# A hybrid encoder layer on one core: re-splitting weights at each use instead of parking the split pair, one weight load for both attentions' up products, one merged attention kept on chip

## The chip, the cores and the metric

The kernel runs on one core of one Trainium2 chip. The metric is device time in microseconds (us) of one execution. All figures below come from one profiled execution and from three runs of the kernel before.

## The reference, cut

Two sequences (`x_prompt`, `x_sample`; each 512 tokens by 1024 channels) go through the same layer:

```python
def encoder_layer(x, ...):
    x = x + 0.5 * swiglu(rms_norm(x, ffn1_norm), ...)           # 1024 -> 2816 -> 1024
    proj = rms_norm(x, mix_norm) @ w_in                         # one joint input projection
    aq, ak, av, mq, mk, mv, gate_pre, o_pre, g_att, g_mlstm = split(proj)
    att = gqa_block_attention(rope(norm(aq)), rope(norm(ak)), av)        # 8 heads of 64, width 512
    mem = mlstm_bidirectional(mq, mk, mv, gate_pre, ..., o_pre, head_norm)  # 4 heads of 128, width 512
    merged = sigmoid(g_att) * (att @ w_up_att) + sigmoid(g_mlstm) * (mem @ w_up_mlstm)
    x = x + merged @ w_out                                      # 1024 -> 1024
    x = x + 0.5 * swiglu(rms_norm(x, ffn2_norm), ...)
    return x
# trunk: one such layer, then rms_norm(x, final_norm)
```

All data are fp32. The change lies between the last part of the joint projection and the start of the second FFN: memory heads, the two "up" products, the merge, the output product.

## The kernel before, in words

**Precision.** Every fp32 operand of a product is split into a high and a low float32r half. A product over K blocks of 128 is then three matmuls for each block (high x high, high x low, low x high). Splitting a weight block takes one ScalarE (ACT) copy (L213, or L265 in the FFN), and one VectorE (DVE) subtraction (L214 or L266).

**Stages.** FFN1 and the joint projection treat both sequences together, by a seven-product scheme of the Strassen kind: sums of weight blocks (`gu_left_a`, `gu_left_b`, `gu_left_c`) are multiplied by sums of activations (`xc`, made by `right_sums`). So does the second FFN. Its first products (L307 into `mm` and others) need the split gate block (L265, L266) and `xc`; L315 and L322 empty them. Between these stages the mixer treats the two sequences one after the other: `m0` and `m1`, objects of the class `Mixer`. Its steps:

- A memory head is `mem_head` (scores at L1178, exponentials at L1192, products with the values at L1231) and `mem_out` (transposes at L1223, squares, the norm). The norm's sums go through transposes on PE (L177), two short steps on GpSimd (POOL; L165, L167, which gives `rs`), and PE again, which spreads `rs` over the partitions (L187). Each head reads four tables of exponents from HBM (`box` from `ebuf`, L1137), to which POOL adds a mask for the first sequence (L1141).
- `merge_att(d)`: for each of eight blocks of 128 output channels, 12 matmuls of `w_up_att` with the attention (L731), then (1 + gate row) times that product (L1099), written to `mgbuf` in HBM (L1100).
- `merge_mem(d)`: 12 matmuls of `w_up_mlstm` with the memory; the gated result is added to the row read back from `mgbuf`, and split.
- `out_unit(d)`: 24 matmuls of `w_out`; the residual row comes from `xbuf` (L1249), is added (L1250) and written to `x2buf` (L1251). Beside the second sequence's out units, `prep2` reads the first sequence's `x2buf` rows (L1496), norms them (L628), writes them to `xnbuf` (L1498) and splits them into `xc` (L252, L253).

**Weights.** `load_w` is called twice for each up and out block, once for each sequence, with the same key. The first call fetches the raw block (512 KB), splits it, and writes both halves to HBM (`wpark`, 2 x 512 KB, L236). The second call reads both halves back (L228). Raw blocks share four buffers, split pairs four others.

**Order.** A unit is a pair (load, comp); `go` and `fill` issue a unit's load some units ahead of its products. A queue of units is filled in between the steps of the memory heads by `between()`. A table, `pace = 0, 12, 30`, says how many units are to be out after the first and after the second 24 of these steps. The queue holds one leftover of the joint projection, eight `merge_att` of `m0`, eight of `m1`, eight `merge_mem` of `m0`, eight `out_unit` of `m0`. Then follow eight `merge_mem` and eight `out_unit` of `m1`, then the FFN's first fetch. A scheduler orders instructions by priority (`shifted` changes it), after which each engine works through its own list in order. All large DMAs are issued by SyncE (SP), also in order.

Of the kernel before, what the change touches and what calls it, by code (L numbers as in the profile page):

```python
# [8 lines left out]
F32 = mybir.dt.float32  # L9
# [3 lines left out]
ALU = mybir.AluOpType  # L13
# [3 lines left out]
P = 128  # L17
S = 512
D = 1024
KD = D // P  # L20
# [6 lines left out]
def encoder(ctx, tc, I, outs):  # L27
    nc = tc.nc
# [90 lines left out]
    def f(ap):  # L119
        return ap.bitcast(F32)  # L120
# [16 lines left out]
    def A(shape, dtype=F32, name="a"):  # L137
        return apool.tile(shape, dtype, tag="a", name=nm(name))
# [82 lines left out]
    def load_w(view, key, ahead=60):  # L221


        if key in parked:
            d, shape = parked[key]
            w2 = wpool.tile(shape, F32R, tag="w8", bufs=4, name=nm("w"))
            for i in range(2):
                nc.sync.dma_start(f(w2[:, i]), d[:, i])  # L228
            return w2[:, 0], w2[:, 1]
        raw = fetch_w(view)  # L230
        with shifted(-ahead):
            hi, lo = split_w(raw, V_)
        shape = [P, 2] + list(raw.shape[1:])
        parked[key] = d, _ = dpool.tile(shape, F32, name=nm("wpark")), shape
        for i, t in enumerate((hi, lo)):
            nc.sync.dma_start(d[:, i], f(t))  # L236
        return hi, lo
# [3 lines left out]
    V_ = nc.vector  # L241
# [480 lines left out]
    def proj(view, key, src, n, done):  # L722

        return (lambda: load_w(view, key)), (lambda w: done(proj_w(*w, src, n)))

    def proj_w(wh, wl, src, n, p=None):
        p = p or MM()
        for k in range(n):
            sh, sl = src(k)
            for i, (a, b) in enumerate(((wh, sh), (wh, sl), (wl, sh))):  # L730
                nc.tensor.matmul(p, a[:, k, :], b, start=(k == 0 and i == 0), stop=(k == n - 1 and i == 2))  # L731
        return p
# [109 lines left out]
            if between:  # L842
                between()
    vbuf = [dpool.tile([P, 2, 4, S], F32, name=f"vbuf{s}") for s in range(2)]
    mgbuf = [dpool.tile([P, KD, S], F32, name=f"mgbuf{s}") for s in range(2)]
    abuf = [dpool.tile([P, 4, 2, S], F32, name=f"abuf{s}") for s in range(2)]

    class Mixer:
# [224 lines left out]
        def up_unit(self, part, d, src, done, bank=None, extra=None):  # L1073
            def load():
                if d % 2 == 0:
                    wv = I[("w_up_att", "w_up_mlstm")[part]][0].rearrange("(k p) c -> p k c", p=P)
                    self.wups[part, d // 2] = load_w(wv[:, :, d * P:(d + 2) * P], ("up", part, d))
                if extra:
                    extra()

            def comp(_):
                wu = self.wups[part, d // 2]
                cl = slice((d % 2) * P, (d % 2 + 1) * P)
                done(proj_w(wu[0][:, :, cl], wu[1][:, :, cl], lambda k: (src()[:, k, 0, :], src()[:, k, 1, :]), 4,
                            bank and bank()))
            return load, comp

        def load_att(self):
            self.att = A([P, 4, 2, S], F32R, "att")
            nc.sync.dma_start(f(self.att), abuf[self.s])  # L1090

        def gate_row(self, g, d):
            t = self.ths[g, d] = T2()
            nc.sync.dma_start(t, mgbuf[self.s][:, d, :] if g == "g" else J[0].buf[self.s][g, d])

        def merge_att(self, d):
            def done(pu):
                t = self.ths.pop(("a", d))
                V_.scalar_tensor_tensor(t, t, 1.0, pu, op0=ALU.add, op1=ALU.mult)  # L1099
                nc.sync.dma_start(mgbuf[self.s][:, d, :], t)  # L1100
            return self.up_unit(0, d, lambda: self.att, done, None, lambda: self.gate_row("a", d))

        def merge_mem(self, d):
            def done(pu):
# [6 lines left out]
            return self.up_unit(1, d, lambda: self.mem, done, (PS, PT)[d % 2], lambda: [self.gate_row(g, d) for g in "mg"])  # L1111

        def mem_fetch(self, h):
            qk = self.qks[h] = []
# [129 lines left out]
        def out_unit(self, d, acc, after=None):  # L1244
            s = self.s

            def done(pp):
                xt = T2(F32, "f2")
                nc.sync.dma_start(xt, xbuf[s][:, d, :])  # L1249
                V_.scalar_tensor_tensor(xt, pp, 0.5, xt, op0=ALU.mult, op1=ALU.add)  # L1250
# [5 lines left out]
            return proj(wov[:, :, d * P:(d + 1) * P], ("out", d), lambda k: (self.mh[:, k, :], self.ml[:, k, :]), KD,  # L1256
                        done)

    pin = tc.keep_in_program_order
# [192 lines left out]
    m0.mem_fetch(1)  # L1452
    queue.append((lambda: None, lambda _: j.rest(13)))
    m0.load_att()
    queue.extend(m0.merge_att(d) for d in range(KD))
    m1.load_att()
    queue.extend(m1.merge_att(d) for d in range(KD))
    acc2 = [None, None]
    heads = [(m, h) for m in (m0, m1) for h in range(HM)]
    step = [0]  # L1460
    pace = 0, 12, 30

    def between():
        i, n = divmod(step[0], 24)
# [46 lines left out]
    W += [up.left(j) for j in (1, 2)]  # L1511
# [140 lines left out]
```

## Time and profile before

| | |
|---|---|
| three runs: median (lowest to highest) | 2092.08 us (2089.03 to 2097.18) |
| the profiled execution: time, span | 2092.42 us, 2090.6 us |
| granted TensorE clock, mean | 0.996 |
| busy share of the span: PE, DVE, ACT, POOL | 97%, 78%, 45%, 6% |
| HBM traffic | 298.21 MB read, 170.03 MB written, 224 GB/s |

The profiled execution's time includes the little that lies around its span. A row of a timeline gives the start in us from the span's start, the busy time, the engine, the line, the operation, and result <- operands; in brackets stands how long the engine had stood before it, and for what. "x12" is a count of instructions in a row. In a view of waits, a row says which engine's instruction stood for which other's, the total in us, how often, and the longest. PE is the matmul engine, PEclk its granted clock as a share of full speed.

### The profile page before, as it was taken

How to read it: one execution, taken by the hardware profiler on the slowest of the kernel's cores; microseconds unless marked ns; L12 is line 12 of the kernel's file. 1: busy time of each engine (PE TensorE's matmuls, PEld its weight loads, DVE VectorE, ACT ScalarE, POOL GpSimd, SP SyncE). 2: the span in 40 equal slices, each digit the busy share in tenths (PEclk: the TensorE clock that was granted, in tenths of full speed). 3: DMA queues.
4: the chain of work that ended last, by engine and by line, in shares of the span. 5: the costliest groups of instructions: out<-in, count | busy, mean ns of one | idle time of the engine just before them, and what ended most of it. 6: DMA issues, size and time to landing. Idle time of an engine off the chain costs nothing.

```text
span 2090.6 us, 27261 instructions
## 1 busy us (share of the span) xinstructions
PE 2036.4 (97%) x9320; PEld 1661.9 (79%) x9320; DVE 1639.6 (78%) x2790; ACT 943.2 (45%) x1751; POOL 135.4 (6%) x147
## 2 busy tenths in 40 slices
PE   8999999999999999999999888998999999999998
PEld 6888888888888777888887666876888888888887
DVE  6888988786797698479987679555888888795796
ACT  7544444442225565435555657323544444443222
POOL 1000000001002220010100110201000000000010
PEclk9999999999999999999999999999999999999999
DMA  8655655699765656664536889998756555598753
GB/s 283 201 179 184 198 175 178 209 341 353 267 230 200 192 152 201 235 216 127 151 112 213 277 298 310 318 313 277 220 167 223 177 186 182 174 354 336 278 191 116
DMA packets 333435, 470.07 MB, mean 225 GB/s; under 512 B 22160, under 2 KB 187040, under 8 KB 331504
## 3 DMA queue, kind: packets, MB, share of 16 engines
q1 hardware_dynamic: 332704, 467.06, 67.0%
q0 software_dynamic: 592, 1.27, 0.3%
q8 instruction: 73, 1.20, 0.2%
q14 instruction: 66, 0.54, 0.1%
HBM read 298.21 MB, written 170.03 MB: 224 GB/s over the span
## 4 chain that ended last, share of the span: by engine, by line
PE 64%; DVE 6%; DMA 5%; ACT 1%; issue 1%; POOL 1%; SPq 0%; POOLq 0%; DVEq 0%; ACTq 0%
PE mm L307 15%; PE pss L307 9%; PE mm L563 8%; PE pst L307 6%; PE pst L563 4%; PE pss L563 4%; PE mm L731 3%; PE mm L715 3%; PE pso L563 3%; PE pso L1057 1%; PE pss L1030 1%; PE pst L1049 1%; PE pss L715 1%; DMA f<-x2buf 1%; PE pst L731 1%
## 5 line engine op out<-in xcount | busy, mean ns | idle before, releaser
L307 PE MATMUL mm<-xc,w 128*128 128x512 f32 x2064 | 515.9, 393 | 10.7 <-ACT w L265 8.4
L307 PEld LDWEIGHTS mm<-xc,w 128*128 128x128 f32 x2064 | 386.1, 189 | 93.5 <-ACT w L265 10.1
L307 PE MATMUL pss<-xc,w 128*128 128x512 f32 x1056 | 256.1, 391 | 0.0
L307 PE MATMUL pst<-xc,w 128*128 128x512 f32 x1056 | 253.8, 389 | 0.2 <-ACT t L342 0.2
L307 PEld LDWEIGHTS pss<-xc,w 128*128 128x128 f32 x1056 | 196.9, 188 | 46.9 <-DVE t L338 6.2
L307 PEld LDWEIGHTS pst<-xc,w 128*128 128x128 f32 x1056 | 198.1, 188 | 41.8 <-ACT t L342 0.6
L265 ACT ACTIVATE w<-t 128x512 fp32r<-128x512 f32 x232 | 141.4, 628 | 181.1 <-issue 55.2
L266 DVE TENSOR_TENSOR w<-t,w 128x512 fp32r<-128x512 f32 x232 | 158.1, 697 | 55.2 <-ACT w L265 52.8
L563 PE MATMUL mm<-rt,w 128*128 128x512 f32 (+1 forms) x819 | 189.1, 384 | 0.0
L563 PEld LDWEIGHTS mm<-rt,w 128*128 128x128 f32 x819 | 151.5, 188 | 29.7
L307 PE MATMUL pss<-xc,f 128*128 128x512 f32 x528 | 126.8, 389 | 0.0
L307 PEld LDWEIGHTS pss<-xc,f 128*128 128x128 f32 x528 | 99.1, 188 | 20.6
L632 ACT ACTIVATE w<-wr 128x512 fp32r<-128x512 f32 x72 | 45.2, 632 | 138.2 <-PE pso L563 71.2
L632 ACT ACTIVATE w<-t 128x512 fp32r<-128x512 f32 x82 | 51.6, 632 | 114.4 <-PE pst L563 69.0
L266 DVE TENSOR_TENSOR w<-wr,w 128x1024 fp32r<-128x1024 f32 x58 | 71.8, 1237 | 35.7 <-ACT w L265 35.7
L563 PE MATMUL pss<-rt,w 128*128 128x512 f32 x396 | 93.7, 389 | 0.0
L563 PE MATMUL pst<-rt,w 128*128 128x512 f32 x396 | 93.7, 389 | 0.0
L715 PE MATMUL mm<-w,xc 128*128 128x512 f32 (+1 forms) x432 | 91.2, 358 | 2.1 <-DVE xs L581 1.4
L563 PEld LDWEIGHTS pss<-rt,w 128*128 128x128 f32 x396 | 74.3, 188 | 15.4
L563 PEld LDWEIGHTS pst<-rt,w 128*128 128x128 f32 x396 | 74.3, 188 | 15.4
L715 PEld LDWEIGHTS mm<-w,xc 128*128 128x128 f32 x432 | 72.0, 188 | 13.8 <-DVE xs L581 1.6
L731 PE MATMUL mm<-mh,w 128*128 128x512 f32 x256 | 80.4, 391 | 0.0
(342 smaller groups left out, 3465.7 us busy)
## 6 DMA issues: line engine op xcount, KB each, us to landing
rt<-rbuf SPq DMA_DIRECT2D x154, 512.0 KB, 5.8
wr<-in_ffn_w_gate_dram SPq DMA_DIRECT2D x62, 512.0 KB, 5.6
rbuf<-tab SPq DMA_DIRECT2D x102, 256.0 KB, 4.1
wr<-in_w_in_dram SPq DMA_DIRECT2D x50, 512.0 KB, 4.6
wpark<-w SPq DMA_DIRECT2D x48, 512.0 KB, 4.9
w<-wpark SPq DMA_DIRECT2D x48, 512.0 KB, 6.7
wr<-in_ffn_w_up_dram SPq DMA_DIRECT2D x44, 512.0 KB, 4.7
rbuf<-f SPq DMA_DIRECT2D x72, 256.0 KB, 3.7
```

Of the source, the lines that this page charges most:

```text
L265: pin(nc.scalar.activation(t[:, 0], src, AF.Copy))
L266: pin(V_.tensor_tensor(t[:, 1], src, f(t[:, 0]), op=ALU.subtract))
L307: nc.tensor.matmul(p, a[:, k, :], xt[:, b, k, :], start=(first and k == 0 and i == 0), stop=(k == HK_ - 1 and i == 2), skip_group_check=True)
L563: nc.tensor.matmul(p, u[:, a, d * P:(d + 1) * P], r[:, b, ts], start=(first and q == 0 and k == 0), stop=(q == len(us) - 1 and k == 2), sk ...
L632: nc.scalar.activation(hi, src, AF.Copy)
L715: nc.tensor.matmul(p[b][:, :N], a[:, bs], w_[:, kl, :], start=(k == 0 and i == 0), stop=(k == KD - 1 and i == 2))
L731: nc.tensor.matmul(p, a[:, k, :], b, start=(k == 0 and i == 0), stop=(k == n - 1 and i == 2))
L1030: nc.tensor.matmul(p, self.qT[:, h, b * P:(b + 1) * P], self.kv[:, hk * 2 + j, :], start=(j == 0), stop=(j == 1))
L1049: nc.tensor.transpose(p[:, b * P:(b + 1) * P], Ps[b][:, kb * P:(kb + 1) * P], ident)
L1057: nc.tensor.matmul(po, self.Vst[:, kv_, hk, :], w, start=(kv_ == 0 and i == 0), stop=(kv_ == 3 and i == 1))
```

## The change

It does six things:

1. `load_w` with `None` for a key returns the fresh split, and parks nothing. Up and out blocks are loaded with `None`, so every use fetches the raw block and splits it.
2. `merge_atts(d)` loads one block of `w_up_att`, both sequences' gate rows, and runs both sequences' 12 matmuls from that load.
3. The merged attention of `m0` goes to a tile on chip (`m0.mg`, 1024 x 512) and is read from there. That of `m1` still goes through `mgbuf`.
4. The queue holds eight `merge_atts` in place of sixteen `merge_att`, and `pace` becomes `0, 7, 23`.
5. The first fetch of the FFN's gate and up block, and the gate block's split, move from behind the last out unit of `m1` to behind its fifth.
6. The block of `w_up_mlstm` is loaded in `merge_mem`'s own load.

```diff
@@ load_w
         with shifted(-ahead):
             hi, lo = split_w(raw, V_)
+        if key is None:
+            return hi, lo
...
-    mgbuf = [dpool.tile([P, KD, S], F32, name=f"mgbuf{s}") for s in range(2)]
+    mgbuf = dpool.tile([P, KD, S], F32, name="mgbuf")
...
+        def up_load(self, part, d):
+            if d % 2 == 0:
...
+                self.wups[part, d // 2] = load_w(wv[:, :, d * P:(d + 2) * P], None)
...
             nc.sync.dma_start(f(self.att), abuf[self.s])
+            if not self.s:
+                self.mg = A([P, KD, S], F32, "mg")
...
-        def merge_att(self, d):
-            def done(pu):
-                t = self.ths.pop(("a", d))
+        def merge_att(self, d, w):
+            src = self.att
+            pu = proj_w(*w, lambda k: (src[:, k, 0, :], src[:, k, 1, :]), 4)
+            t = self.ths.pop(("a", d))
+            if self.s:
                 V_.scalar_tensor_tensor(t, t, 1.0, pu, op0=ALU.add, op1=ALU.mult)
-                nc.sync.dma_start(mgbuf[self.s][:, d, :], t)
-            return self.up_unit(0, d, lambda: self.att, done, None, lambda: self.gate_row("a", d))
+                nc.sync.dma_start(mgbuf[:, d, :], t)
+            else:
+                V_.scalar_tensor_tensor(self.mg[:, d, :], t, 1.0, pu, op0=ALU.add, op1=ALU.mult)
...
-                t, mg = self.ths.pop(("m", d)), self.ths.pop(("g", d))
+                t, mg = self.ths.pop(("m", d)), self.ths.pop(("g", d)) if self.s else self.mg[:, d, :]
...
-            return proj(wov[:, :, d * P:(d + 1) * P], ("out", d), ...
+            return proj(wov[:, :, d * P:(d + 1) * P], None, ...
...
-    queue.extend(m0.merge_att(d) for d in range(KD))
     m1.load_att()
-    queue.extend(m1.merge_att(d) for d in range(KD))
+
+    def merge_atts(d):
+        def load():
+            for m in (m0, m1):
+                m.gate_row("a", d)
+            return m0.up_load(0, d)
+
+        def comp(w):
+            for m in (m0, m1):
+                m.merge_att(d, w)
+        return load, comp
+
+    queue.extend(merge_atts(d) for d in range(KD))
...
-    pace = 0, 12, 30
+    pace = 0, 7, 23
...
-    go(*[m1.out_unit(d, acc2, prep2) for d in range(KD)])
+    last = [m1.out_unit(d, acc2, prep2) for d in range(KD)]
+    go(*last[:5])
+    raw0 = gu_fetch(*[I[n][0].rearrange("(k p) c -> p k c", p=P) for n in ("ffn2_w_gate", "ffn2_w_up")], 0)
+    W = [gu_left_a(raw0[0])]
+    go(*last[5:])
     flush()
...
-    raw0 = up.fetch(0)
-    W = [gu_left_a(raw0[0])]
     up.begin(0, W[0])
```

The diff does not tell where the instructions land. SP's list shrinks from 1242 rows to 1188, and moves at the end of the second sequence's output. Before, the list reads there (`wr` is a raw weight buffer, `f` a row of 512 tokens):

```order
L1251 DMA x2buf_119<-f_1672_12528 128x512
L1249 DMA f_1677_12569<-xbuf_117 128x512
L1496 DMA f_1679_12576<-x2buf_118 128x512
L1249 DMA f_1681_12607<-xbuf_117 128x512
L1496 DMA f_1683_12614<-x2buf_118 128x512
L206 DMA wr_12638<-in_ffn_w_gate_dram 128x8x128
L1251 DMA x2buf_119<-f_1677_12569 128x512
L1498 DMA xnbuf<-f_1679_12576 128x512
L1498 DMA xnbuf<-f_1683_12614 128x512
L206 DMA wr_12640<-in_ffn_w_up_dram 128x8x128
L206 DMA wr_12677<-in_ffn_w_gate_dram 128x8x128
L1251 DMA x2buf_119<-f_1681_12607 128x512
```

The first gate load stands there between the sixth and the seventh of the eight writes to `x2buf` (L1251). In the changed kernel the same engine's list has the first gate and up loads much earlier (lines of the changed kernel: L1257, L1259, L1515, L1517 for L1249, L1251, L1496, L1498):

```order
L206 DMA wr_12350<-in_w_out_dram 128x8x128
L206 DMA wr_12393<-in_ffn_w_gate_dram 128x8x128
L1517 DMA xnbuf<-f_1628_12258 128x512
L1257 DMA f_1659_12473<-xbuf_116 128x512
L206 DMA wr_12395<-in_ffn_w_up_dram 128x8x128
L1515 DMA f_1661_12480<-x2buf_117 128x512
L206 DMA wr_12400<-in_w_out_dram 128x8x128
L1517 DMA xnbuf<-f_1634_12301 128x512
L1517 DMA xnbuf<-f_1640_12344 128x512
L1257 DMA f_1665_12516<-xbuf_116 128x512
L1259 DMA x2buf_118<-f_1624_12250 128x512
```

The last row is the first of the eight writes. Two of the four raw buffers hold the FFN's gate and up block from here on; raw `w_out` loads, which were reads of `wpark` before, go through the same four.

The end of that list in the changed kernel:

```order
L1259 DMA x2buf_118<-f_1644_12380 128x512
L206 DMA wr_12617<-in_ffn_w_gate_dram 128x8x128
L1259 DMA x2buf_118<-f_1653_12430 128x512
L206 DMA wr_12622<-in_ffn_w_gate_dram 128x8x128
L1259 DMA x2buf_118<-f_1659_12473 128x512
L206 DMA wr_12696<-in_ffn_w_gate_dram 128x8x128
L1259 DMA x2buf_118<-f_1665_12516 128x512
L206 DMA wr_12750<-in_ffn_w_gate_dram 128x8x128
L1259 DMA x2buf_118<-f_1669_12554 128x512
```

Four more gate blocks now alternate with the last five writes. On PE the work beside the memory heads moves. Before, the first head's norm stands so (`att_10066` is the first sequence's attention, and L731 its up product; `pst` <- `ident,t` at L177 are the sums, `ident,rs` at L187 the spread norm):

```order
L731 MATMUL mm_10299<-att_10066,w_10176 128x512 x4
L731 MATMUL mm_10385<-att_10066,w_10176 128x512 x12
L731 MATMUL mm_10452<-att_10066,w_10377 128x512 x2
L177 MATMUL pst_10279<-ident,t_1260_10276 128x128 x4
L731 MATMUL mm_10452<-att_10066,w_10377 128x512 x7
L1178 MATMUL pss_10337<-qk_10314 128x512
L1178 MATMUL pss_10362<-qk_10314 128x512
L731 MATMUL mm_10452<-att_10066,w_10377 128x512 x3
L187 MATMUL pst_10289<-ident,rs_10286 128x128
```

The changed kernel has there, with `att_10065` for the first sequence and `att_10068` for the second (L733 and L1186 are L731 and L1178 of before):

```order
L733 MATMUL mm_10428<-att_10065,w_10254 128x512 x2
L1239 MATMUL pso_10071<-t_1250_10155,Vm_9891 128x512
L733 MATMUL mm_10428<-att_10065,w_10254 128x512 x7
L733 MATMUL mm_10442<-att_10068,w_10254 128x512 x2
L1186 MATMUL pss_10344<-qk_10212 128x512 x2
L177 MATMUL pst_10194<-ident,t_1254_10191 128x128 x4
L1186 MATMUL pss_10344<-qk_10212 128x512
L733 MATMUL mm_10442<-att_10068,w_10254 128x512 x6
L187 MATMUL pst_10204<-ident,rs_10201 128x128
```

Fewer up products stand ahead of L187, and fewer between L177 and L187. In POOL's list six mask adds stand ahead of this head's `rs`; before, there were five. At the third head's norm PE has before:

```order
L731 MATMUL mm_10807<-att_10066,w_10660 128x512 x5
L177 MATMUL pst_10703<-ident,t_1345_10700 128x128 x4
L1178 MATMUL pss_10764<-qk_10741 128x512
L1178 MATMUL pss_10789<-qk_10741 128x512
L187 MATMUL pst_10713<-ident,rs_10710 128x128 x4
```

And in the changed kernel:

```order
L733 MATMUL mm_10683<-att_10068,w_10545 128x512 x5
L177 MATMUL pst_10647<-ident,t_1335_10644 128x128 x4
L733 MATMUL mm_10683<-att_10068,w_10545 128x512
L1186 MATMUL pss_10724<-qk_10701 128x512 x3
L1186 MATMUL pss_10749<-qk_10701 128x512 x3
L733 MATMUL mm_10796<-att_10065,w_10545 128x512 x12
L733 MATMUL mm_10810<-att_10068,w_10545 128x512 x12
L187 MATMUL pst_10657<-ident,rs_10654 128x128
```

A whole merged unit, 24 matmuls, now stands between the sums and L187, where two score matmuls stood.

More of the change, by code (lines that the diff above doesn't have):

```diff
@@ L1071, in attend @@
                     nc.sync.dma_start(abuf[self.s][:, h // 2, i, :], f(w))
[L1073 to L1086, printed above, removed]
+        def up_load(self, part, d):
+            if d % 2 == 0:
+                wv = I[("w_up_att", "w_up_mlstm")[part]][0].rearrange("(k p) c -> p k c", p=P)
+                self.wups[part, d // 2] = load_w(wv[:, :, d * P:(d + 2) * P], None)
+            wu = self.wups[part, d // 2]
+            cl = slice((d % 2) * P, (d % 2 + 1) * P)
+            return wu[0][:, :, cl], wu[1][:, :, cl]
         def load_att(self):
@@ L1110, in done @@
                 split(t, self.mh[:, d, :], self.ml[:, d, :])
-            return self.up_unit(1, d, lambda: self.mem, done, (PS, PT)[d % 2], lambda: [self.gate_row(g, d) for g in "mg"])
+            return load, comp
         def mem_fetch(self, h):
@@ L1255, in out_unit @@
             wov = I["w_out"][0].rearrange("(k p) c -> p k c", p=P)
-            return proj(wov[:, :, d * P:(d + 1) * P], ("out", d), lambda k: (self.mh[:, k, :], self.ml[:, k, :]), KD,
+            return proj(wov[:, :, d * P:(d + 1) * P], None, lambda k: (self.mh[:, k, :], self.ml[:, k, :]), KD,
                         done)
@@ L1454, in encoder, with load, comp @@
     m0.load_att()
-    queue.extend(m0.merge_att(d) for d in range(KD))
     m1.load_att()
-    queue.extend(m1.merge_att(d) for d in range(KD))
+    def merge_atts(d):
+        def load():
+            for m in (m0, m1):
+                m.gate_row("a", d)
+            return m0.up_load(0, d)
+        def comp(w):
+            for m in (m0, m1):
+                m.merge_att(d, w)
+        return load, comp
+    queue.extend(merge_atts(d) for d in range(KD))
     acc2 = [None, None]
```

9 lines of the change are left out of this document (7 added, 2 removed).

## The prediction

> **What bounds the kernel now.** I read the page first: span and busy shares.
>
> ```profile
> span 2090.6 us, 27261 instructions
> PE 2036.4 (97%) x9320; PEld 1661.9 (79%) x9320; DVE 1639.6 (78%) x2790; ACT 943.2 (45%) x1751; POOL 135.4 (6%) x147
> ```
>
> The profiled execution took 2092.42 us, 1.8 more than its span and 0.3 over the median of the runs, 2092.08. TensorE (PE) is busy for 97%, and the edit takes no product away. So time can only come out of the 54 us in which PE stands, or out of slow clock. The second view is busy time by stretch, cut where the edited work lies: memory heads of the first sequence, heads of the second, first output projection, second merge and output, start of the second FFN.
>
> ```profile
> core 0: us, PE busy (x) PEld busy (x) DVE busy (x) ACT busy (x) POOL busy (x), PEclk, DMA share, GB/s
> 1172.00:1248.00 76.00, 65.33 (x309) 51.08 (x308) 57.47 (x147) 46.07 (x114) 13.62 (x12) 0.98 0.81 271
> 1248.00:1312.00 64.00, 56.99 (x274) 43.98 (x273) 56.09 (x133) 44.17 (x105) 2.53 (x4) 1.00 0.96 315
> 1312.00:1369.00 57.00, 55.82 (x261) 45.00 (x260) 25.88 (x39) 16.28 (x25) 12.91 (x12) 1.00 0.94 312
> 1369.00:1431.00 62.00, 61.86 (x274) 50.71 (x273) 29.76 (x45) 13.91 (x22) 7.74 (x6) 1.00 0.89 305
> 1431.00:1461.00 30.00, 22.97 (x93) 17.79 (x93) 18.47 (x26) 14.43 (x21) 1.50 (x3) 0.89 0.91 266
> ```
>
> The DMA share is 0.81 to 0.96 everywhere, yet from 1312 to 1431 PE hardly stands: the copies of the split weights load the transfer engines there and delay nothing. PE stands in the heads (10.7 and 7.0 us) and at the FFN's start (7.0, at a clock of 0.89). The third view, PE's waits from 1120 to 1500, says for what (us in total, times, longest):
>
> ```profile
> PE pst L187 <- POOL rs L167: 8.5, 4, 3.6
> PE mm L307 <- ACT w L265: 6.8, 2, 5.1
> PE pso L1231 <- ACT t L632: 3.7, 3, 1.7
> PE mm L731 <- DMA w<-wpark: 2.9, 2, 2.6
> ```
>
> The largest is the norm of a memory head (L187 spreads what POOL computes at L165 and L167), then the FFN's first weights. Only 2.9 us are a wait for a parked weight.
>
> **The change, part by part.**
>
> *Transfers.* These rows give size and time to landing:
>
> ```profile
> wpark<-w SPq DMA_DIRECT2D x48, 512.0 KB, 4.9
> w<-wpark SPq DMA_DIRECT2D x48, 512.0 KB, 6.7
> R<-ebuf SPq DMA_DIRECT2D x16, 256.0 KB, 3.5
> box<-ebuf SPq DMA_DIRECT2D x16, 256.0 KB, 5.1
> mgbuf<-t SPq DMA_DIRECT2D x16, 256.0 KB, 3.8
> ```
>
> Of the 48 parked writes and 48 reads, 32 each belong to the up and out weights (8 + 8 + 16) and go: 64 x 0.52 MB = 33.6 MB. Eight writes and eight reads of mgbuf go too, 4.2 MB. Twelve raw loads come (4 memory up, 8 out): 6.3 MB. That is 31.5 MB and some 70 issues of SP less. By themselves these are worth only the two waits for w<-wpark: **-2.9 us**. Bounds: 0, if the same matmul then waits for the split, to -2.9.
>
> *Added splits.* The rows of one such split (L265, L266), of the other DVE work of an output unit and of 24 matmuls in a row:
>
> ```profile
> 1434.84 1.06 ACT L265 ACTIVATE w<-wr 128x1024 fp32r<-128x1024 f32 x1 [0.48 <-DMA wr<-in_ffn_w_gate_dram]
> 1435.93 1.23 DVE L266 TENSOR_TENSOR w<-wr,w 128x1024 fp32r<-128x1024 f32 x1 [0.84 <-ACT w L265]
> 1437.07 0.69 DVE L1250 SCALAR_TENSOR_TENSOR f<-mm,f 128x512 f32<-128x512 f32 x1
> 1422.85 0.75 DVE L628 SCALAR_TENSOR_TENSOR f<-f,gain,R 128x512 f32<-128x512 f32 x1 [6.23 <-DMA f<-x2buf]
> 1424.31 0.69 DVE L253 TENSOR_TENSOR xc<-f,xc 128x512 fp32r<-128x512 f32 x1
> 1373.58 2.89 PE L731 MATMUL pst<-mem,w 128*128 128x512 f32 x12
> 1376.30 2.88 PE L731 MATMUL pss<-mem,w 128*128 128x512 f32 x12
> ```
>
> Twelve raw tiles are split again for the second sequence: one ACT copy (1.06) and one DVE subtraction (1.23) each, so 12.7 us of ACT and 14.8 of DVE. They fall between 1312 and 1431, where DVE is idle for 119 - 55.6 = 63 us. Twelve matmuls start within 2.72 us (1373.58 to 1376.30), 0.227 each; an output unit takes PE 24 x 0.227 = 5.44 us, and DVE then has 0.69 + 0.75 + 0.69 + 1.23 = 3.4 us of work. I take 0; with that cover gone, +14.8. Of the merge of the second sequence, 8 x 12 matmuls take 21.8 us against some 21.5 of DVE by my count of its queue: 0 to +1.5.
>
> *The FFN's start.* The gate block is now fetched and split after five of eight output units. Before, it looks so (the SPq row is an issue; the split that follows is the pair of rows above):
>
> ```profile
> 1426.56 0.43 SPq L206 DMA_DIRECT2D wr<-in_ffn_w_gate_dram  x1
> 1435.95 5.41 PE L307 MATMUL mm<-xc,w 128*128 128x512 f32 x12 [5.09 <-ACT w L265]
> 1442.10 5.96 PE L307 MATMUL mm<-xc,w 128*128 128x512 f32 x25 [0.30 <-ACT f L315]
> 1460.94 4.40 PE L307 MATMUL mm<-xc,w 128*128 128x512 f32 x18 [1.74 <-ACT w L265]
> ```
>
> The load is issued at 1426.56, lands 8 us later, and PE has stood 5.09 us. Twelve matmuls then take 5.41 us, where twelve start within 2.72 at full clock: the slow clock costs 2.7 more. 1.74 and 0.30 follow. In the new SP queue the first gate load stands ahead of the write of the first output row, the next four among the last writes. Each then has at least one unit of 5.44 us to land and be split. So 5.09 + 2.7 + 0.30 + 1.74 = **-9.8 us**; bounds -9.8 and 0.
>
> The Trainium skill (TensorE: Matmul & The Clock Gate, section on the HAM clock gate) says that some 3.4 us of idleness halve the clock until about 3.4 us of work have gone by. By that rule a closed gap gives back 1.7 us, not 2.7, and the sum would be 1.0 smaller. The trace agrees in kind: after 5.09 us the matmuls slow down, by more than the rule has.
>
> What is late next is DVE, which must make the other operand sums before PE's first product into pss:
>
> ```profile
> 1449.22 0.69 DVE L193 COPY R<-pst 128x512 f32<-128x512 f32 x1
> 1491.51 1.48 DVE L266 TENSOR_TENSOR w<-t,w 128x512 fp32r<-128x512 f32 x2
> 1496.45 2.88 PE L307 MATMUL pss<-xc,w 128*128 128x512 f32 x12
> ```
>
> DVE needs 43 us from the copy at 1449.22 to the weight at 1491.51 plus 1; PE came 4 us after. With PE 9.8 earlier, the copy follows PE's transposes and comes 8 earlier too (L1250, which it depends on, no longer stands behind the split of 1435.93), and three gate splits of 1.23 leave this stretch. That leaves 4 + 8 + 3.7 - 9.8 = 6 us of cover: 0, at worst +2.
>
> *Heads.* Merging both attentions in one unit, with a pace of 7 and 23 instead of 12 and 30, redistributes what PE does beside a head.
>
> ```profile
> 1174.33 1.58 ACT L1192 ACTIVATE t<-box,st 128x128 f32<-128x128 f32 x5 [0.69 <-PE pso L1231]
> 1177.85 0.38 SPq L1137 DMA_DIRECT2D box<-ebuf  x1
> 1182.51 1.91 POOL L1141 TENSOR_TENSOR box<-box,tab 128x512 f32<-128x512 f32 x1 [31.43 <-DMA box<-ebuf]
> 1186.77 0.32 PE L187 MATMUL pst<-ident,rs 128*128 128x128 f32 x1 [3.60 <-POOL rs L167]
> 1221.73 0.65 PE L187 MATMUL pst<-ident,rs 128*128 128x128 f32 x4 [1.75 <-POOL rs L167]
> 1223.61 0.63 PE L1223 MATMUL pst<-ident,t 128*128 128x128 f32 x4 [1.24 <-DVE t L1207]
> 1284.76 0.60 PE L177 MATMUL pst<-ident,t 128*128 128x128 f32 x4
> 1288.40 0.32 PE L187 MATMUL pst<-ident,rs 128*128 128x128 f32 x1 [2.12 <-POOL rs L167]
> ```
>
> First head: from the Joint's last product to L187, PE had 36 up matmuls, now 20: 16 x 0.227 = 3.6 us less. POOL has one mask add more ahead of the norm, 1.28 at least (1.91 in the row). But its transfer was issued at 1177.85, 1.9 us after the last reader (1174.33 + 1.58), behind other issues that now stand behind it. Net 3.6 + 1.28 - 1.9 = **+3.0**; bounds 0 and +5.5 (two adds of 1.91, no earlier issue). Third head: 2 matmuls stood between the sums (L177) and L187, now 31, so 1.75 + 1.24 go: **-3.0**; bounds 0 and -3.0. Fifth and sixth: 1284.76 to 1288.40 shows that the norm takes 3.6 us. The fifth head keeps 7 matmuls of 15 (0.45 + 1.6 of cover, so +1.6, from none), the sixth gets 10 for 4 (0.45 + 2.3, so 0.9 instead of 2.12): **+0.4**; bounds -1 and +3. The last head's norm keeps 6 matmuls and four transposes as cover: 0.
>
> **Sum.** -2.9 - 9.8 + 3.0 - 3.0 + 0.4 = -12.3. 2092.4 - 12.3 = **2080 us**, 12 below the runs' median. Added up with their bounds most terms would not fall together; I give this case 2074 to 2086.
>
> **Rivals.**
>
> *The heads eat it.* A merged unit fetches two gate rows at once and the next unit's two before it runs, from the eleven rows that odd heads use too. If a row comes free late, SP stands, and with it the masks and q, k behind it. For it: DVE is busy 56.1 of 64 us from 1248 to 1312. Against it: half of the mgbuf writes, which wait there as well, are gone. One wait of 1.2 us (the row of 1223.61) for each of eight units gives +9.6: 2090.
>
> *Lighter transfers help more.* Same-sized reads of ebuf land in 5.1 us in the heads and 3.5 in a quieter stage. If five POOL, ACT and DVE chains there get 1.6 us shorter, 8 more go: 2072. The Trainium skill (DMA: Bandwidth & Descriptors, section Latency and other measured facts) states a mechanism for it: HBM access takes longer under load. The two ebuf rows agree in direction.
>
> *Slower.* Two of the four raw buffers now hold the FFN's gate and up block from the fifth output unit on, so output units 5 to 7 and gate blocks 1 to 9 share two. A buffer's round is load, ACT, DVE: 8.0 + 1.06 + 1.23 = 10.3 us for two units of 5.44. It decides when the round passes 10.9. An in-order queue that issues each load one unit late makes it 15.7, 2.4 late per block: 12 blocks cost 29 us, 2109. Against it: gate blocks already ran with two buffers, at one wait of 1.74.
>
> *Nothing changes.* The gate load moves up, but its split stays behind waiting work on DVE: the 5.09 remain, 2090 to 2092.
>
> **How the numbers follow.** This kernel's runs (2089.03 to 2097.18) cannot tell 0.5%, 10.5 us, from no change; the line is 2081.6. Chances: the sum 0.58, heads 0.17, lighter transfers 0.15, slower 0.06, nothing 0.04. Of the first, six in ten lie under the line (0.35), and all of the transfers' case: faster 0.50. Same: 0.23 + 0.17 + 0.04 = 0.44. Slower 0.06. The range 2071 to 2091 leaves out the slower case and a tail on either side.
>
> **What would show it.** Right: PE goes from the last output matmul into the FFN's first product with no wait over 0.5 us at a clock of 1.00; the waits for w<-wpark in this stretch are gone; DVE in the two output stretches some 15 us busier with PE above 98%; the first head's wait near 7 us, the third's under 1. Wrong: a wait of PE for a split weight (L213, L214) in the output units, a gap ahead of the FFN's first product into pss, or waits in the heads that add up to more than the 18 us of before.

## The result, and the profile after

The changed kernel took 2077.69 us (median of 5 runs, 2072.27 to 2078.61) against 2095.36 for the kernel before in the same comparison: ratio 0.9913, 95% interval 0.989 to 0.9936. The forecast was 2080. The profiled execution took 2078.2 us, 14.2 less than the one of before. (Medians of the kernel before lie between 2089.7 and 2095.4 from one comparison to the next, so below only ratios and stretches of a trace are compared.)

The page of the changed kernel: span, busy shares, and the bytes that crossed HBM.

```profile
span 2076.4 us, 27167 instructions
PE 2036.5 (98%) x9320; PEld 1664.9 (80%) x9320; DVE 1652.3 (80%) x2802; ACT 954.3 (46%) x1763; POOL 135.4 (7%) x147
HBM read 285.63 MB, written 151.16 MB: 210 GB/s over the span
```

PE does the same 2036.5 us of work in 14.2 us less; DVE has 12.7 us more, ACT 11.1: the added splits. Busy time by stretch, cut as in the prediction's table (heads of the first sequence, of the second, first output, second merge and output, the FFN's start; columns as there):

```profile
1174.00:1248.00 74.00, 69.98 (x340) 56.10 (x340) 60.99 (x154) 49.17 (x122) 10.91 (x12) 0.98 0.64 209
1248.00:1308.00 60.00, 53.28 (x238) 41.89 (x238) 50.11 (x117) 38.37 (x89) 2.71 (x4) 0.91 0.53 162
1308.00:1365.00 57.00, 55.69 (x261) 44.56 (x259) 31.75 (x51) 22.02 (x35) 14.04 (x12) 1.00 0.59 186
1365.00:1427.00 62.00, 62.00 (x276) 51.29 (x277) 44.26 (x59) 25.09 (x34) 9.41 (x6) 1.00 0.73 233
1427.00:1457.00 30.00, 30.00 (x138) 24.48 (x137) 23.51 (x34) 18.17 (x28) 1.27 (x2) 1.00 0.87 266
```

The last row has PE at 30.00 of 30 us with a clock of 1.00, where it had 22.97 at 0.89. In the four rows above it the DMA share (next to last column), which lay between 0.81 and 0.96, lies between 0.53 and 0.73. In the second row PE still stands 6.7 us, now at a clock of 0.91. The two largest of PE's waits from 1120 to 1500, and the rows that the prediction asked for:

```profile
PE pst L187 <- POOL rs L167: 9.9, 5, 4.0
PE pso L1239 <- ACT t L634: 1.5, 4, 0.7
```

```profile
1183.48 0.47 PE L187 MATMUL pst<-ident,rs 128*128 128x128 f32 x1 [2.98 <-POOL rs L167]
1289.60 0.48 PE L187 MATMUL pst<-ident,rs 128*128 128x128 f32 x1 [3.96 <-POOL rs L167]
1426.84 3.33 PE L309 MATMUL mm<-xc,w 128*128 128x512 f32 x14
1482.32 2.88 PE L309 MATMUL pss<-xc,w 128*128 128x512 f32 x12
```

The norms' waits are still there (9.9 us against 8.5), in part on other heads. The FFN's first product (1426.84) has no wait in front of it, its first product into pss neither. Two of the prediction's signs came out otherwise: the first head waits 2.98 us and not near 7, and DVE is 20 us busier in the two output stretches (76.0 against 55.6) and not 15.

To compare kernels I use two stretches, both between rows of PE. "Heads" is from the first memory head's first scores to the second sequence's first out product: 256.6 us before (1130.55 to 1387.18), 250.9 after (1132.41 to 1383.32). "Start" is from there to the FFN's first product into pss: 109.3 before (1387.18 to 1496.45), 99.0 after (1383.32 to 1482.32). Together -16.0; the rest of the trace lost 1.8, ahead of the heads. One trace fixes the heads to some 2 to 3 us only: kernels that differ in nothing but the FFN's fetch read 256.6 and 254.0 there (before, experiment 1), and 250.9 and 248.8 (changed, experiment 2). The start takes 98.9 to 99.3 us in all eight traces in which PE waits for nothing there.

### The profile page after: what moved, and what is told of

The parts are those of the page before. It is cut to its first block, busy times and chain, and to the rows that moved or that the text cites. A ratio compares the mean times of both kernels' runs of the same rounds, so it can differ in the third digit from the quotient of the medians.

```text
span 2076.4 us, 27167 instructions
## 1 busy us (share of the span) xinstructions
PE 2036.5 (98%) x9320; PEld 1664.9 (80%) x9320; DVE 1652.3 (80%) x2802; ACT 954.3 (46%) x1763; POOL 135.4 (7%) x147
## 2 busy tenths in 40 slices
DMA packets 332347, 438.60 MB, mean 211 GB/s; under 512 B 21072, under 2 KB 196192, under 8 KB 330416
## 4 chain that ended last, share of the span: by engine, by line
PE 86%; DVE 6%; DMA 4%; ACT 2%; issue 1%; POOL 1%; SPq 0%; DVEq 0%; POOLq 0%; ACTq 0%
PE mm L309 20%; PE pss L309 17%; PE pst L309 11%; PE mm L565 8%; PE mm L733 5%; PE pst L565 4%; PE pss L565 4%; PE mm L717 3%; PE pso L565 3%; PE pso L1059 1%; PE pst L1051 1%; PE pss L1032 1%; PE pss L717 1%; PE pst L733 1%; PE pss L1186 1%
## 5 line engine op out<-in xcount | busy, mean ns | idle before, releaser
L267 ACT ACTIVATE w<-wr 128x1024 fp32r<-128x1024 f32 x58 | 61.4, 1058 | 50.2 <-PE pst L309 21.6
```

The lines of the kernel that those rows point to most:

```text
L267: pin(nc.scalar.activation(t[:, 0], src, AF.Copy))
```

## The experiments

All were timed against the kernel before; ratios carry 95% intervals.

**1 and 2: the move of the FFN's fetch, alone and left out.** Edit of the first, on the kernel before:

```diff
-    go(*[m1.out_unit(d, acc2, prep2) for d in range(KD)])
+    last = [m1.out_unit(d, acc2, prep2) for d in range(KD)]
+    go(*last[:5])
+    raw0 = gu_fetch(...)
+    W = [gu_left_a(raw0[0])]
+    go(*last[5:])
```

> The kernel before with only the FFN's first fetch and gate split moved to behind the fifth out unit of the second sequence; weights are still parked. Theory (the start of the FFN was late because its first load was issued late, and nothing else): the 5.09 us wait ahead of the FFN's first product, the slow matmuls behind it and the 1.74 go, so 10 us less than before (ratio 0.995), and the mixers' part keeps its time within 1.5 us. Rival (the move only pays because reads of parked weights no longer stand in SP's queue and on the transfer engines): with the reads still there a wait of 2 us or more stays ahead of that product, and the gain is 5 us or less.

Measured: ratio 0.9997 (0.9987 to 1.0006): nothing. Rows of SP (an issue) and PE, and the stretch up to the FFN's first product:

```profile
1402.35 0.43 SPq L206 DMA_DIRECT2D wr<-in_ffn_w_gate_dram  x1
1417.05 1.22 PE L731 MATMUL mm<-mh,w 128*128 128x512 f32 x2 [3.01 <-DMA w<-wpark]
1435.69 3.35 PE L307 MATMUL mm<-xc,w 128*128 128x512 f32 x14
1386.00:1435.00 49.00, 45.99 (x190) 37.25 (x190) 17.27 (x21) 9.13 (x15) 7.71 (x6) 0.93 0.84 281
```

The gate load was issued 24 us earlier than before, and the FFN's first product did not wait, as the theory said. But now an out unit waits 3.01 us for its parked pair, and PE runs at a clock of 0.93: the start takes 107.2 us instead of 109.3. Reads of parked halves that SP issued at 1403.04 and 1404.79 before come at 1407.69 and 1412.46 here, behind the FFN's 1 MB. The wait changed its place.

The opposite edit, on the changed kernel (the fetch put back behind the last unit):

> The changed kernel with the FFN's first fetch put back behind the last out unit. Theory (two independent parts): the FFN's start costs what it cost before (wait of 4.5 to 5.5 us, slow matmuls, a second wait of 1 to 2 us), so 10 us slower than the changed kernel, 5 to 6 faster than before (ratio 0.997 to 0.998). Rival (lighter transfers also bring the first gate load in sooner): the wait is 3 us or less, and the kernel is 8 us or more faster than before.

Measured: ratio 0.9929 (0.9916 to 0.9941), 2077.59 us: as fast as the changed kernel.

```profile
1396.74 0.45 SPq L206 DMA_DIRECT2D wr<-in_ffn_w_gate_dram  x1
1425.66 3.33 PE L309 MATMUL mm<-xc,w 128*128 128x512 f32 x14
```

With the fetch where it was in the code, SP issues the gate load at 1396.74, 30 us earlier than the 1426.56 of before, and nothing waits. So the move in the code is worth nothing, with parked weights or without. My theory for the largest term fell in both.

**3 and 4: the other two parts alone.** Re-splitting on the kernel before:

```diff
+        if key is None:
+            return hi, lo
...
-  load_w(wv[...], ("up", part, d))       -> load_w(wv[...], None)
-  proj(wov[...], ("out", d), ...)        -> proj(wov[...], None, ...)
```

> The kernel before with only the parking of up and out weights taken away; queue, pace, both mgbufs and the FFN's fetch as before. Theory A (as forecast: the transfers were worth only the 2.9 us of waits for parked weights): those go, and the third head's norm, which now has 12 matmuls of cover by the order of the instructions instead of 2, loses 1.7 us: 3 to 5 us less than before. From the last joint product to the first head's spread norm it takes 17 us, as before. Theory B (the copies of the weights delayed the heads' own loads): that stretch gets 3 to 5 us shorter beyond the matmuls moved, and the kernel is 7 us or more faster.

Measured: ratio 0.9937 (0.9925 to 0.9948). Heads 251.6 us, start 99.0: one part of the change gives most of the gain. Theory B's number for the whole came in; its place did not: from the last joint product (1168.54) to the first head's spread norm (1186.16) it still took 17.6 us.

Experiment 4 is the changed kernel with memory up and out weights still parked, and the fetch put back:

> The kernel before with only the merged attention units, the first merged attention on chip and the pace 0, 7, 23; memory up and out weights still parked, the FFN's fetch as before. Theory A (order decides in the heads): from the last joint product to the first head's spread norm some 12.4 us, as in the changed kernel, against 17.4 before; third head without a wait, sixth head's norm waits some 4 us; in sum 2 to 5 us less than before. Theory B (the traffic decides): that stretch stays at 15 us or more, with 0 to 2 us gained or lost in all.

Measured: ratio 0.994 (0.9929 to 0.9952). That stretch took 13.5 us, the sixth head's norm waited 3.27, both near theory A; heads 252.1 us. But the gain is above A's 2 to 5, since the start fell too, to 103.8. The edit left the FFN's fetch where it was in the code, yet SP's list did not: the first gate load stands ahead of all out units.

```profile
1335.42 1.43 SPq L206 DMA_DIRECT2D wr<-in_ffn_w_gate_dram  x1
```

So this run too has an early fetch, which the edit did not ask for. PE waits for no weight in its start, but 2.63 us for the squares of the last output row (DVE, L158), with slow matmuls behind. Experiments 3 and 4 gain 13 and 12 us, and experiment 2, which has both edits, 14: the gains overlap almost wholly. Experiment 4 also moves 12.6 MB less than before (457.48 against 470.07 MB), so that it is no test of the order alone.

**5 and 11: out weights and up weights apart.** Only `("out", d)` becomes `None`:

> The kernel before with only the out weights re-split at each use; up weights still parked, all else as before. On PE the order of instructions in the memory heads is that of before. Theory (the FFN's late start comes from the second sequence's reads of parked out weights, 1 MB for each out unit, which keep SP's queue and the transfer engines behind): from the second sequence's first out product to the FFN's first product into pss 99 us instead of 109.3, no wait of PE there, and the heads as before within 2 us: 8 to 11 us less (ratio 0.995 to 0.996). Rival (the traffic of all weights together matters, so the up weights' half must go too): 104 us or more there, and 5 us or less gained.

Only the up weights' key becomes `None`:

> The kernel before with only the up weights re-split; out weights parked, all else as before. Theory (two parts that add up: up weights act in the heads, out weights at the FFN's start): from the first head's scores to the second sequence's first out product 251 to 253 us (256.6 before, 258.5 with only the out weights re-split), and 107 to 110 us from there to the FFN's first product into pss as before: 4 to 6 us less than before in all (ratio 0.997 to 0.998). Rival (each half brings what both bring, since either relieves SP): that second stretch falls to 102 us or less, ratio 0.995 or less.

Measured: out weights 0.996 (0.9946 to 0.9974), heads 258.5, start 100.4; up weights 0.9965 (0.9952 to 0.9978), heads 251.5, start 104.3. So the heads gain by the up weights only, and the start by either: most by the out weights (-8.8 us), but 4.9 by the up weights. The start of 104.3 lies between theory and rival: the FFN's first load is issued at 1409.46 there, 17 us sooner than before, with its order in SP's list moved, and PE waits 2.88 us for the squares of the last output row.

**6 and 9: the bytes put back, without parking.** Both are experiment 3 with scratch copies that nobody reads. The first copied rows of `w_out` from HBM to HBM beside each out unit:

> The kernel with re-split up and out weights (pace and merging as before), and with the same bytes put back as copies that nobody waits for: each out unit also copies rows of w_out from HBM to HBM, 1 MB for the first sequence and 512 KB for the second. Theory H1 (the volume on the transfer engines made the FFN late): PE waits 3 us or more between the second sequence's first out product and the FFN's first product into pss, that stretch takes 104 us or more, and the kernel is 5 to 10 us slower than without the copies. Theory H2 (not the bytes, but that reads of parked pairs go into the four pair buffers that PE frees, so that SP stands in front of them and everything behind waits): the stretch stays within 1 us of 99, and the kernel within 2 us of that without the copies.

It tested nothing at the place it was meant for. The copies had nothing to wait for, and the scheduler put them at the kernel's start (24 issues, first at 37.5 us, last at 137.6; columns: least, median and greatest ns of an issue, first and last start):

```profile
L1265 SPq DMA_DIRECT2D dead<-in_w_out_dram x24: 489/587/1305, 37.5 to 137.6; - x24
```

Start 99.0, as without them. The ratio was 0.9969 (0.9958 to 0.9979); the trace is 6.0 us longer up to the first head's scores (1135.82 against 1129.85). Of these PE lost some 3 where the copies ran: it is busy for 97.5 of the 101 us from 37 to 138 at a DMA share of 0.94, against 100.4 at 0.65 in experiment 3. The second tied the copies to the output rows:

```diff
                 nc.sync.dma_start(x2buf[s][:, d, :], xt)
+                for i in range(2 if s else 4):
+                    nc.sync.dma_start(dead[s][:, d, i, :], xt)
```

> The kernel with re-split up and out weights, with the bytes put back at the place they had: each output row is also written to a scratch tensor that nobody reads, four more times (1 MB) for the first sequence and twice (512 KB) for the second, right behind its own write, so that SP waits for nothing new. (The copies of the run before this one had nothing to wait for and ran at the kernel's start.) Theory H1 (volume): from the second sequence's first out product to the FFN's first product into pss 104 us or more instead of 99, with a wait of PE of 3 us or more; 5 to 10 us slower than without the writes (ratio to before 0.996 to 1.0). Theory H2 (pair buffers that PE frees): 101 us or less, and the kernel within 2 us of 0.9937.

Measured: ratio 1.0015 (1.0003 to 1.0026). The whole gain is gone, with no weight parked.

```profile
1431.17 0.32 SPq L1254 DMA_DIRECT2D x2buf<-f  x1
1432.53 0.66 SPq L206 DMA_DIRECT2D wr<-in_ffn_w_gate_dram  x1
1438.05 0.90 PE L177 MATMUL pst<-ident,R 128*128 128x128 f32 x3 [2.70 <-DVE R L158]
1439.84 1.22 PE L309 MATMUL mm<-xc,w 128*128 128x512 f32 x2 [0.89 <-ACT w L267]
1465.13 5.06 PE L309 MATMUL mm<-xc,w 128*128 128x512 f32 x21 [1.65 <-ACT w L267]
1391.00:1439.00 48.00, 45.25 (x198) 36.61 (x196) 29.90 (x37) 18.32 (x26) 8.54 (x6) 0.99 0.92 295
1439.00:1500.00 61.00, 58.22 (x245) 46.87 (x246) 47.78 (x67) 36.48 (x56) 1.26 (x2) 0.96 0.94 287
```

The gate load is late again (1432.53). PE waits again: 2.70 us for the squares of the last output row, then 0.89 and 1.65 for gate weights. The start takes 108.6 us, at a DMA share of 0.92 to 0.94, and the heads, in which the first sequence's writes lie, 258.2. Without the writes the same stretch of experiment 3 reads so:

```profile
1420.46 0.32 SPq L1253 DMA_DIRECT2D x2buf<-f  x1
1381.00:1425.00 44.00, 44.00 (x196) 36.42 (x195) 27.82 (x35) 17.52 (x24) 10.11 (x6) 1.00 0.66 209
1425.00:1480.00 55.00, 55.00 (x247) 45.27 (x246) 46.23 (x68) 34.36 (x54) 1.26 (x2) 1.00 0.87 272
```

This decides against H2: added bytes alone, without a pair buffer, bring the late start back. How they act is less clear, since the order of SP's list moved with them: the first gate load stands behind the seventh of the eight last writes with the scratch writes, behind the first in experiment 3, behind the second in experiment 2, behind the sixth before. The seventh write itself is hardly late with the scratch writes: 39.8 us after the first out product (1391.41 to 1431.17), against 39.0 in experiment 3 (1381.47 to 1420.46). So the gate load is late here by its place in the list, which is fixed before the kernel runs. Before, the sixth write was issued after 37.0 us, against 33.5 in experiment 3: there some 3.5 us are delay on the chip.

Read together, the starts separate a part that is not the place. An out unit moves 1 MB of parked pair, or 512 KB of raw block with or without 512 KB of scratch writes. With 1 MB the start takes 109.3 us (first gate load issued 39.4 us after the first out product), 108.6 (after 41.1, experiment 9), 107.2 (after 16.3, experiment 1), 104.3 (after 29.8, experiment 11) and 103.8 (long before it, experiment 4). With 512 KB it takes 98.9 to 100.4. So in these runs some 5 us of the 10 stay wherever that load stands; the other 5 differ with its place and with what it overtakes. No run has light out units and a late gate load, which would show what the place alone costs.

**10: the same in the heads.** Experiment 3 with scratch writes of merged rows, 10 MB:

> The kernel with re-split up and out weights, with extra scratch writes of the merged rows beside the memory heads instead: two for each attention row of the first sequence, one for each of the second, two for each memory row of the first, 10 MB in all, what the parked up weights moved there in excess of the raw ones. Theory H1 (bytes and SP issues delay the heads' loads): from the first head's scores to the second sequence's first out product 256 us or more instead of 251.6, and 4 us or more slower in all. Theory H2 (the pair buffers, which parked reads and the heads' q and k share, delay them): within 2 us of the kernel without the writes. The FFN's start keeps 99 us by both.

Measured: ratio 0.9971 (0.996 to 0.9983); heads 257.5 us, start 99.3. H1 again. The order of PE's instructions shifted a little with the added writes, and ACT stood once for 1.4 us for a row that a scratch write still read, so a part of the 6 us may be order or held rows. Heads as one window each, of experiments 3, 10 and of the kernel before:

```profile
1129.85:1381.47 251.62, 234.89 (x1099) 186.40 (x1100) 190.54 (x412) 144.58 (x319) 34.14 (x30) 0.99 0.73 238
```

```profile
1131.82:1389.36 257.54, 237.37 (x1098) 187.51 (x1099) 191.22 (x411) 144.59 (x319) 30.45 (x30) 0.98 0.84 273
```

```profile
1130.55:1387.18 256.63, 235.82 (x1099) 186.05 (x1099) 180.44 (x403) 135.45 (x310) 31.96 (x30) 0.99 0.90 306
```

PE stands for 16.7 us in the first, for 20.2 and 20.8 in the others, and its busy time, which grows where the clock is slow, differs by up to 2.5. The share of the whole stretch does not foretell its length: the heads take 251.5 us at 0.79 (experiment 11), 252.1 at 0.81 (experiment 4) and 258.5 at 0.84 (experiment 5), but 258.2 at 0.76 in experiment 9.

**7: light transfers, short reach.** Experiment 3 with the raw block in one of the four pair buffers:

> The kernel with re-split up and out weights, but the raw block is loaded into the first half of a buffer of the four pair buffers, not of the four raw ones: light transfers, with the short reach of the parked reads (the raw load of a unit waits for what PE has done two units before). By the order of instructions the FFN's first gate loads come very early here, so the test is in the out units. H2 (the reach of the buffers decides): PE waits 3 us or more in all for split weights in the two sequences' merge and out units, and the kernel is 4 us or more slower than the re-split one. H1 (the bytes decide): no wait over 0.5 us there, and within 2 us of the re-split one.

Measured: ratio 0.9976 (0.9964 to 0.9988), 8 us slower than experiment 3, though PE nowhere waits directly for a split weight.

```profile
1131.61:1393.73 262.12, 238.66 (x1099) 189.34 (x1100) 191.76 (x412) 145.13 (x320) 30.13 (x30) 0.97 0.72 231
```

The time went in the heads, 262.1 us at a share of only 0.72. (The FFN's first gate load is issued at 1130.90 there, so that its start of 98.9 us says nothing of a late first load.) So buffers can cost as much as bytes there; the heads' q and k take pair buffers too, which I hold to be the way, but no run isolates it. In the out units H2's wait did not come. The run leaves open how much of the parked kernel's loss in the heads was buffers; experiment 10 shows that bytes alone can bring a loss of that size.

**8: another pace.** `pace = 0, 10, 24` on the changed kernel:

> The changed kernel with pace 0, 10, 24 instead of 0, 7, 23. By the order of instructions the norms of the eight heads have 25, 27, 39, 15, 3, 27, 67, 77 matmuls between the sums and the spread norm, instead of 7, 17, 31, 52, 7, 10, 75, 93. Theory (a head's wait is its norm less its cover): the first head's wait of 2.98 and the sixth's of 3.96 with the slow matmuls behind them go, the fifth's grows from 1.19 to 2 to 3: 5 to 8 us less than the changed kernel (ratio to before 0.989 to 0.991). Rival (VectorE, busy for most of the heads, sets their time; waits only move to other instructions): within 2 us of the changed kernel.

Measured: ratio 0.9927 (0.9911 to 0.9942), 2076.82 us: as the changed kernel. The waits in the heads are others:

```profile
PE pso L1239 <- ACT t L634: 4.8, 6, 2.5
PE pst L187 <- POOL rs L167: 3.2, 2, 2.2
PE pss L1186 <- DVE f L1202: 2.1, 1, 2.1
```

The norms' waits fell from 9.9 to 3.2 us, and ACT's and DVE's results are waited for instead; heads 251.4 against 250.9. The rival held: counting the matmuls that stand in front of a norm foretells which head waits, not what the heads take.

**12: no parking at all.** The input projections' weights re-split as well:

```diff
-  load_w([win_v[...] ...], ("in", cols[0], k0), ahead)
+  load_w([win_v[...] ...], None, ahead)
```

> The changed kernel with the last parked weights, those of the input projections (24 writes and 24 reads, 21.5 MB between 650 and 900 us), re-split as well: 15.8 MB less there. Theory (bytes cost time only where the transfer engines are nearly full and something waits behind them in SP's queue; between 600 and 900 us their share is 0.52 to 0.69 and PE's only wait for a parked weight there is 0.5 us): within 2 us of the changed kernel, ratio to before 0.992 to 0.994. Rival (fewer bytes are worth about as much per MB anywhere; 31.5 MB brought 14 us): 5 to 8 us less than the changed kernel.

Measured: 2074.26 us, ratio 0.9912 (0.9898 to 0.9926): the lowest median of all kernels here, 3 us under the changed kernel's, but by the ratio (0.9913) its equal. From 650 to 900 us the DMA share falls from 0.65 to 0.48 and PE's busy time hardly moves (the changed kernel, then this one):

```profile
650.00:900.00 250.00, 244.10 (x1238) 196.45 (x1237) 185.37 (x340) 142.09 (x281) 43.18 (x53) 1.00 0.65 210
```

```profile
650.00:900.00 250.00, 244.36 (x1242) 197.41 (x1241) 197.35 (x351) 150.99 (x292) 46.98 (x54) 1.00 0.48 149
```

Here 15.8 MB less left PE where it was, within 0.3 us. By the ratio the theory held, if a little beyond its 0.992; the medians, which come from two comparisons, lie 3 us apart, between theory and rival. In the traces this kernel reaches the first head's scores 3.5 us sooner than the changed one (1128.91 against 1132.41), but kernels with the same code up to there differ by as much (1128.13 to 1133.30), so that the 3 us are not shown to be its own.

## Why the prediction was right in the number and wrong in the cause

- **The step that failed** is the sentence behind the table of stretches: "the copies of the split weights load the transfer engines there and delay nothing". I looked at who waits inside the stretch. The delay was paid at its end, in the FFN's start: it takes 100.4 us instead of 109.3 when only the out weights' copies go (experiment 5), and 108.6 when scratch writes take their place (experiment 9). The sizes on the page could have warned me: an output unit of the second sequence moves a pair (2 x 512 KB) and four rows (256 KB each), 2.1 MB in 5.44 us of PE, 385 GB/s; 305 were reached from 1369 to 1431. Re-split it is 1.57 MB, 289 GB/s. That is an estimate of the demand, not of its price: experiments 4 and 11 have the same 2.1 MB and lose half as much.

 The Trainium skill (DMA: Bandwidth & Descriptors, section Specifications) gives some 358 GB/s of HBM for a core. This trace does not show that ceiling: it moved 376 over 18 us just ahead of the out units.

```profile
1369.00:1387.18 18.18, 18.18 (x83) 14.87 (x82) 15.57 (x25) 5.66 (x9) 0.00 (x0) 1.00 1.03 376
```

- **The FFN's start**, -9.8: measured -10.3, the size right. It was the 5.09, the slow clock and the 1.74 that went. The reason given, the earlier fetch, is worth nothing measurable, alone or in company (experiments 1 and 2). The re-split out weights bring most of it by themselves (experiment 5: -8.8).
- **Transfers**, -2.9: the bytes were right (31.5 MB; the two pages differ by 470.07 - 438.60), the price was not. Alone the re-splitting is worth 0.63%, 13 us (experiment 3), of which the start has 10 us.
- **The heads**, -2.5 with the waits for parked weights: measured -5.7. The first head was put at +3.0; its waits fell by 1.5, since its tables came earlier. These rows of POOL show it (the first mask no longer waits for its table):

```profile
1177.13 1.31 POOL L1149 TENSOR_TENSOR box<-box,tab 128x512 f32<-128x512 f32 x1 [22.33 <-ACT t L1200]
1182.00 0.30 POOL L165 TENSOR_SCALAR rs<-cs 128x4 f32<-128x4 f32 x1
```

 The third head's wait went, as forecast. The sixth was put at 0.9 and waited 3.96, with slow matmuls behind: DVE reduced its sums (L179) at 1287.41, 4 us after PE had made them, where it had taken 1 us before; the merged rows and the head's own rows stand in front of it on DVE. Experiment 8 says that such single terms don't add up to the heads' time anyway.
- **Added splits** at 0, and 6 us of cover for DVE ahead of pss: right. DVE has 44.26 instead of 29.76 us in the last output stretch, and PE stands nowhere in it.
- **The rivals.** "Lighter transfers help more" was right that bytes were worth more than 2.9, but not in its reason. The tables that were to land 1.6 us sooner in the heads land in 4.9 us, where it had been 5.1 (the like reads of the quieter stage took 3.5 before and 3.6 after):

```profile
box<-ebuf SPq DMA_DIRECT2D x16, 256.0 KB, 4.9
```

 And it added its gain to the fetch's 9.8 instead of putting it in its place. "The heads eat it", "slower" and "nothing changes" did not come.

Two errors cancelled: 9.8 us were booked on an edit worth nothing, and the edit worth them was booked at 2.9. That 2080 came so near to 2077.69 was luck in its largest term.

## What to carry to other kernels

When the transfer engines are nine tenths busy and no engine waits, look at the end of the stretch, at the first loads behind it in the same in-order queue: moving such a load forward in the code can move the wait to what it overtook, as in experiment 1. Work out bytes per unit over the time of a unit before calling transfers hidden; here units of 2.1 MB in 5.44 us went with starts of 103.8 to 109.3 us, units of 1.57 MB with 99.0 to 100.4. Read the lists of instructions of a test as well as its edit: added or removed bytes moved the first load in SP's list, too. When a change has several parts, price each as if the others were absent: two of these parts each gave most of the gain, and one gave none.

## What the runs showed of the hardware that I had not expected

- A short wait can cost twice its length. In experiment 1 a wait of 3.01 us in the out units was followed by matmuls starting up to twice as far apart: 49.6 us from the first out product to the FFN's first, against 43.5 with no wait, so 3.1 us more than the wait itself. PE's clock was 0.50 from 1417 to 1420 and 0.55 from 1420 to 1423. The Trainium skill (TensorE: Matmul & The Clock Gate, section on the HAM clock gate) says that after an idle window of some 3.4 us the clock is halved until some 3.4 us of work have gone by; as an estimate from that, 1.7 us are lost. This trace lost more, as the 5.09 us of before did (2.7).
- Re-reading a raw block of 512 KB and splitting it again (1.06 us of ACT, 1.23 of DVE) was cheaper than reading back 1 MB, though DVE was busy for 78% of the kernel: from 1312 to 1431 DVE was idle for 63 of 119 us while the DMA share was 0.89 to 0.94. Where the share was 0.65 (experiment 12) it made no measurable difference.
